# A streaming encoder step: gate operands one set ahead, sample rows in spent activations, native steps, third split buffers and a leaner scan

## The chip, the cores and the metric

The kernel is one program on one core of a Trainium2 chip. Its time is device microseconds of that core, from the launch to the end; a profiled execution also leaves a trace, whose span (first to last instruction) is a little shorter than the time. The engines are TensorE (PE; its weight loads are PEld), VectorE (DVE), ScalarE (ACT), GpSimd (POOL) and the queues that issue DMA (SP for plain loads and stores, POOL for gathers).

## What is computed

384 token rows (256 of a prompt, 128 of eight sample streams) of width 1024 go through two layers. Layer 0 mixes with a Mamba-2 scan in 8 groups of 4 heads, layer 1 with sliding-window attention; after each stands a PEER block, in which each token has 8 heads with 16 experts each out of 16384:

```
y = ssd_scan(xs, dt, A, B, C, state)                     # layer 0, per group
y = y + xs * d_skip                                      # one factor per head
y = rmsnorm(y * silu(z)) @ w_out
...
eid, gate = top16 of (q1 @ sub_k1 + q2 @ sub_k2)         # PEER, both layers
act = gelu(einsum('tkd,td->tk', u_tab[eid], x))
out = einsum('tk,tkd->td', gate * act, v_tab[eid])
```

## The kernel before

**Split products.** A float32 operand is cut in two fp32r parts: ScalarE casts raw to hi (L105), VectorE subtracts hi from raw into lo (L106). A product is three matmuls, hi x hi, hi x lo and lo x hi (`gemm_cols` L125, `gemm_rows` L134). raw has three buffers, hi and lo two each. A native product takes the float32 operands as they are; a native matmul is two instructions in the trace.

**The scan** (`mamba`, L209). For each of the 8 groups: four tiles of the input projection with their convolution (`conv_tile`), `decay`, `gate`, `tokens`; and, one group later, `states`, `outputs`, `turn` and `carry` of the group before. `outputs` adds the skip term xs * d_skip as a matmul with a diagonal tile dg (L483) into the same bank as the four head products (L487). `carry` adds each sample stream's new state: eight matmuls (L523) over 128 rows, each with a copy of B in which all but one stream's 16 rows are zero (`decay`, L453).

**The PEER block** (`peer`, L847) handles prompt tokens densely and sample tokens by gathers.
- 128 u steps (`u_step` L1130): step e2 loads 512 KB of the u table and writes gelu scores of 256 prompt tokens to G[e2 // 64][:, e2 % 64]. Steps in NATIVE (L47; only in the first 64) use raw and a float32 copy xf of the tokens. Beside the first 64 steps stands the routing (top 16 of the sub-key scores, on VectorE).
- Gates (`w_step` L1143): 32 sets for each half of G. A set builds one-hot operands ob, og and oa on VectorE and ScalarE, multiplies them (L1168) and scales G by the result (L1170). The sets of half 0 stand beside u steps 64 to 127, those of half 1 beside v steps 0 to 63.
- 128 v steps (`v_step` L1175): step e2 loads 512 KB of the v table, splits it and the scores (phi, plo), and adds 12 matmuls of 512 columns to four banks.
- Sample products (`u_item` L1104): for each of 128 columns of expert numbers a gather of 128 rows of u (512 KB) and a product with the sample rows xg on VectorE, at RATES (L54) per step in the three stretches of 64 steps.
- Quads (`v_quad` L1117): 32 quads of four gathered row sets of v; a quad is eight native matmuls on column tiles of 32 (L1126), one each 3.75 v steps from step 2 (QUADS). The gathered rows lie in seven buffers (gv, gath).
- At the end of the v steps h comes back from DRAM (L1265), for the residual sum.

What is written with `pin` keeps its order; the rest a scheduler puts in order per engine when the program is built. Each engine and each queue then runs its list in that order.

## Time and profile before

| | us |
|---|---|
| three runs | 2578.8, 2582.8, 2591.1 |
| median | 2582.8 |
| profiled execution, its own time | 2576.9 |
| its span | 2575.2 |
| TensorE busy | 2425.7 |
| VectorE busy | 1927.6 |
| ScalarE busy | 1313.5 |

The stages, in us from the span's start: scan and its output product to 401, queries of the first PEER block to 487, u steps to 715 and 927, v steps to 1175 and 1386, attention to 1561, and the second PEER block with queries to 1646, u steps to 1876 and 2087, v steps to 2343 and 2567. A stage is read by the busy time of its engines against its length: an engine whose busy time is the length sets it; where none is near, waits do.

### The profile page before, as it was taken

The numbers are of one execution on the slowest core, as the hardware profiler recorded it, in microseconds if no ns is written. First come the engines' busy times: TensorE is split into PE (matmuls) and PEld (weight loads), VectorE is DVE, ScalarE is ACT, GpSimd is POOL, SyncE is SP. The second block draws the span as 40 slices with busy tenths as digits, with TensorE's granted clock in tenths as the row PEclk, the third lists the DMA queues.
The fourth block names the chain that finished last, engine by engine and source line by source line (L and its number), as shares of the span: only waits on it lengthen the run. The fifth ranks groups of instructions, "written<-read, shape, count | busy, mean of one in ns | idle before, by whom it ended". The sixth has DMA issues, their size and how long they took to land. (4 is left out here: it accounts for less than half of the span.)

```text
span 2575.2 us, 45047 instructions
## 1 busy us (share of the span) xinstructions
PE 2425.7 (94%) x16816; PEld 2055.6 (80%) x16816; DVE 1927.6 (75%) x4206; ACT 1313.5 (51%) x2522; POOL 683.2 (27%) x749
## 2 busy tenths in 40 slices
PE   8999999999899999999998998999899999999998
PEld 7999988988789976666666878998789976667666
DVE  5877746989989988765455656989989988765445
ACT  5756524433456666554444544443456665554444
POOL 2222200033332244432331100033332244433331
PEclk9999999999999999999999989999999999999999
DMA  5545434478888899988886314478788898888886
GB/s 183 181 168 178 147 128 148 146 263 276 266 297 285 296 323 334 350 306 307 318 319 208 125 42 157 140 270 274 263 294 286 294 333 330 339 302 305 302 315 231
DMA packets 179117, 645.62 MB, mean 251 GB/s; under 512 B 24193, under 2 KB 26097, under 8 KB 176241
## 3 DMA queue, kind: packets, MB, share of 16 engines
q1 hardware_dynamic: 99632, 366.90, 40.6%
q0 software_dynamic: 79264, 275.84, 31.1%
q8 instruction: 132, 2.16, 0.3%
q14 instruction: 89, 0.72, 0.1%
HBM read 626.43 MB, written 18.06 MB: 250 GB/s over the span
## 5 line engine op out<-in xcount | busy, mean ns | idle before, releaser
L105 ACT CAST hi<-raw 128x1024 fp32r<-128x1024 f32 (+1 forms) x616 | 641.5, 1042 | 650.5 <-PE bank L131 425.7
L106 DVE TENSOR_TENSOR lo<-raw,hi 128x1024 fp32r<-128x1024 f32 (+1 forms) x616 | 750.0, 1218 | 234.3 <-ACT hi L105 233.2
L1072 POOL DMA_INDIRECT gath<-in_p_u,eidU x256 | 297.8, 1163 | 796.6 <-DVE gath L1109 424.0
L132 PE MATMUL bank<-xhi,lo 128*128 128x256 f32 (+1 forms) x1344 | 408.3, 304 | 12.6 <-DVE lo L106 12.5
L130 PE MATMUL bank<-xhi,hi 128*128 128x256 f32 (+1 forms) x1344 | 404.2, 301 | 4.2 <-ACT hi L105 4.2
L131 PE MATMUL bank<-xlo,hi 128*128 128x256 f32 (+1 forms) x1344 | 398.5, 297 | 0.0
L132 PE MATMUL bank<-qhi,lo 128*128 128x256 f32 (+1 forms) x1152 | 349.0, 305 | 29.7 <-DVE lo L106 29.5
L130 PE MATMUL bank<-qhi,hi 128*128 128x256 f32 (+1 forms) x1152 | 348.3, 303 | 19.6 <-ACT hi L105 12.0
L1109 DVE SCALAR_TENSOR_TENSOR gath<-gath,xg 128x1024 f32<-128x1024 f32 x256 | 311.8, 1218 | 50.2 <-DMA gath<-in_p_u,eidU 50.1
L131 PE MATMUL bank<-qlo,hi 128*128 128x256 f32 (+1 forms) x1152 | 344.3, 299 | 0.0
L143 PE MATMUL bank<-lo,phi 128*128 128x512 f32 x1024 | 331.6, 405 | 6.3 <-DVE lo L106 5.9
L143 PE MATMUL bank<-hi,plo 128*128 128x512 f32 x1024 | 322.7, 397 | 0.0
L143 PE MATMUL bank<-hi,phi 128*128 128x512 f32 x1024 | 291.6, 405 | 16.8 <-ACT hi L105 13.6
L105 ACT CAST phi<-G 128x256 fp32r<-128x256 f32 x256 | 103.4, 405 | 378.7 <-PE bank L143 264.9
L1072 POOL DMA_INDIRECT gv<-in_p_v,eidT x180 | 203.6, 1131 | 326.0 <-PE bank L1126 277.2
L132 PEld LDWEIGHTS bank<-xhi,lo 128*128 128x128 f32 x1344 | 255.4, 190 | 20.0 <-DVE lo L106 17.6
L143 PEld LDWEIGHTS bank<-hi,phi 128*128 128x128 f32 x1024 | 186.3, 189 | 96.4 <-ACT hi L105 41.0
L130 PEld LDWEIGHTS bank<-xhi,hi 128*128 128x128 f32 x1344 | 255.9, 190 | 8.8 <-ACT hi L105 5.2
L131 PEld LDWEIGHTS bank<-xlo,hi 128*128 128x128 f32 x1344 | 255.6, 190 | 0.3
L132 PEld LDWEIGHTS bank<-qhi,lo 128*128 128x128 f32 x1152 | 223.3, 195 | 36.5 <-DVE lo L106 36.2
L130 PEld LDWEIGHTS bank<-qhi,hi 128*128 128x128 f32 x1152 | 223.7, 194 | 23.5 <-ACT hi L105 15.1
L143 PEld LDWEIGHTS bank<-lo,phi 128*128 128x128 f32 x1024 | 187.2, 190 | 66.5 <-DVE lo L106 16.5
(343 smaller groups left out, 3889.1 us busy)
## 6 DMA issues: line engine op xcount, KB each, us to landing
raw<-in_u_t SPq DMA_DIRECT2D x256, 512.0 KB, 4.6
raw<-in_p_v SPq DMA_DIRECT2D x256, 512.0 KB, 5.5
raw<-in_w_in SPq DMA_DIRECT2D x32, 512.0 KB, 4.8
raw<-in_p_w_q SPq DMA_DIRECT2D x32, 512.0 KB, 5.5
s<-in_state_ssm SPq DMA_DIRECT2D x8, 1024.0 KB, 4.8
raw<-in_w_z SPq DMA_DIRECT2D x16, 512.0 KB, 3.8
out_sm_ssm<-s SPq DMA_DIRECT2D x8, 1024.0 KB, 4.2
raw<-in_w_out SPq DMA_DIRECT2D x16, 512.0 KB, 4.3
```

The lines of the kernel that those rows point to most:

```text
L105: act.copy(hi, raw)
L106: dve.tensor_tensor(lo, raw, hi32, op=OP.subtract)
L130: pe.matmul(ps, whi[:, s], xhi[:, k, c0:c1], start=(k == 0), stop=False)
L131: pe.matmul(ps, whi[:, s], xlo[:, k, c0:c1], start=False, stop=False)
L132: pe.matmul(ps, wlo[:, s], xhi[:, k, c0:c1], start=False, stop=(k == KD - 1))
L143: mm = pe.matmul(ps, x, w[:, hf * n:(hf + 1) * n], start=s_, stop=e_)
L1072: pool.indirect_dma_start(out=tile_, out_offset=None, in_=tab, in_offset=bass.IndirectOffsetOnAxis(ap=idx, axis=0))
L1109: pin(dve.scalar_tensor_tensor(tile_, tile_, 1.0, xg[g], op0=OP.mult, op1=OP.mult, accum_out=au[g][:, j:j + 1]))
```

## The change

- **Scan.** The skip term leaves TensorE: `tokens` writes xs * d_skip to y on VectorE, `outputs` adds the other terms to it, and dg is gone. `carry` takes B in two copies (streams of even and of odd number) and runs its eight matmuls on row tiles of 32 partitions, two streams each. `turn` and `carry` stand behind the x tiles, and some instructions are pinned.
- **u steps.** 18 native steps in place of 8 per layer (each third step from 3 to 54); a third hi and lo buffer up to step 55; the copies of the prompt's tokens spread over 8 steps. The rate of sample products is 0.75, 0.75 and 0.8 for 0.95, 0.8 and 0.8. The sample rows xg have one buffer: the second group's rows are loaded when the first group's 64 products are done.
- **Gates.** A set's operands are built one set ahead of its matmuls (`w_prepare`, `w_multiply`).
- **v steps.** 12 native steps (2, 7, ... 57), a third hi and lo buffer up to step 120, a third phi and plo. The gathered rows of v go to parts of G[0] that the v steps have used up, from step 18 on and up to 12 rows ahead. Quads stand at steps 24, 27, 30 and 33, and then two at a time each 6.45 steps. h is loaded by GpSimd's queue at step 121.

```
-TURN = 6
+TURN = 8
-NATIVE = range(4, 58, 7)
+NATIVE = range(3, 56, 3)
+NATIVE_V = range(2, 62, 5)
-RATES = (0.95, 0.8, 0.8)
-QUADS = (2, 3.75)
+W_FIRST = (0, 1)
+RATES = (0.75, 0.75, 0.8)
+QUADS = [24, 27, 30, 33] + [int(37 + 6.45 * (i // 2)) for i in range(28)]
...
+    more, turn_of = {}, {}
+    def ring(n, dt, tag, bufs):
+        if n == D and tag in more:
+            pl, extra = more[tag]
+            turn_of[tag] = (turn_of.get(tag, -1) + 1) % (bufs + extra)
+            if turn_of[tag] >= bufs:
+                return T(pl, [P, n], dt, tag=tag + "x", bufs=extra)
+        return T(stream, [P, n], dt, tag=tag, bufs=bufs)
     def load_raw(src, n=D):
-        raw = T(stream, [P, n], F32, tag="raw")
+        raw = ring(n, F32, "raw", 3)
...
-        hi = T(stream, [P, n], F32R, tag="hi", bufs=2)
-        lo = T(stream, [P, n], F32R, tag="lo", bufs=2)
+        hi = ring(n, F32R, "hi", 2)
+        lo = ring(n, F32R, "lo", 2)
...
-                        self.dg = T(two, [P, 2, P], F32, tag="dg", bufs=1)
-                        for j in range(2):
-                            pool.tensor_scalar(self.dg[:, j], ident, dsk[:, 2 * g + j:2 * g + j + 1], None, op0=OP.mult)
...
-                        self.Bt = Bt = T(two, [P, 2 + NSEQ, P], F32, tag="Bt", bufs=1)
+                        self.Bt = Bt = T(two, [P, 4, P], F32, tag="Bt", bufs=1)
                         act.copy(Bt[:, 0:2], pb[:, 0:2])
-                        for i in range(NSEQ):
-                            act.activation(Bt[:, 2 + i], pb[:, 2], AF.Copy, scale=seqm[:, i:i + 1])
+                        for w in range(2):
+                            act.activation(Bt[:, 2 + w], pb[:, 2], AF.Copy, scale=parm[:, w:w + 1])
...
+                            dve.tensor_tensor(heads(self.y[:, b]), heads(px),
+                                              dsk[:, self.hs].unsqueeze(2).to_broadcast([P, 4, 64]), op=OP.mult)
...
-                            for j in range(2):
-                                pe.matmul(o[:, j * P:(j + 1) * P], self.xs[:, j, b * P:(b + 1) * P], self.dg[:, j],
-                                          start=True, stop=False)
-                                for rr in (2 * j, 2 * j + 1):
-                                    cs = slice(64 * rr, 64 * rr + 64)
-                                    pe.matmul(o[:, cs], self.ab[:, rr, b], self.xdt[:, b, cs], start=False,
-                                              stop=(rr == 2 * j + 1))
+                            for rr in range(4):
+                                cs = slice(64 * rr, 64 * rr + 64)
+                                pe.matmul(o[:, cs], self.ab[:, rr, b], self.xdt[:, b, cs], start=True, stop=True)
...
-                        y12 = y[:, 1:].rearrange("p b (r d) -> p b r d", d=64)
-                        dve.tensor_tensor(y12, pO.rearrange("p b (r d) -> p b r d", d=64),
+                        y = self.y
+                        yo = T(two, [P, 2, 256], F32, tag="yo", bufs=1)
+                        dve.tensor_tensor(yo.rearrange("p b (r d) -> p b r d", d=64),
+                                          pO.rearrange("p b (r d) -> p b r d", d=64),
                                           etok[:, :, self.hs].unsqueeze(3).to_broadcast([P, 2, 4, 64]), op=OP.mult)
-                        dve.tensor_tensor(y[:, 0], self.zs[:, 0], pY[0], op=OP.mult)
+                        dve.tensor_tensor(y[:, 1:], y[:, 1:], yo, op=OP.add)
+                        dve.tensor_tensor(y[:, 0], y[:, 0], pY[0], op=OP.add)
                         dve.tensor_tensor(y[:, 1:], y[:, 1:], pY[1], op=OP.add)
-                        dve.tensor_tensor(y[:, 1:], y[:, 1:], self.zs[:, 1:], op=OP.mult)
+                        dve.tensor_tensor(y, y, self.zs, op=OP.mult)
...
-                        for i in range(NSEQ):
-                            pe.matmul(pss[i // 2][:, i % 2], self.Bt[:, 2 + i], self.xde[:, 2], start=True, stop=True)
+                        for w in range(2):
+                            for q in range(4):
+                                rows = slice(32 * q, 32 * q + 32)
+                                pin(pe.matmul(pss[q][:, w], self.Bt[rows, 2 + w], self.xde[rows, 2],
+                                              start=True, stop=True, tile_position=(32 * q, 0)))
...
-                    if g > 1:
-                        prev.turn()
                     G_.x_tile(0)
                     if g == 1:
                         prev.states()
                         prev.outputs()
+                    elif g:
                         prev.turn()
-                    if g:
                         prev.carry()
                     G_.x_tile(1)
+                    if g == 1:
+                        prev.turn()
+                        prev.carry()
...
-            xg = [T(x0ctx.__enter__(), [P, D], F32, tag="xg0"), T(one, [P, D], F32, tag="xg1")]
...
+            xg = {}
+            def load_group(g):
+                xg[g] = T(one, [P, D], F32, tag="xg", bufs=1)
                 rows = xrow[g]
                 pool.dma_start(xg[g], bass.AP(tensor=rows.tensor, offset=rows.offset, ap=[[0, GR], [D, TG], [1, D]]))
+            load_group(0)
...
-                    if done["u"] == P and n % 7 >= 4:
-                        tile_ = T(one, [P, D], F32, tag="gath", bufs=3)
-                    else:
-                        tile_ = T(pools["gv"], [P, D], F32, tag="gv", bufs=4)
+                    k = 4 * (n % (4 if n < 16 else 8 if n < 64 else 16))
+                    if k + 3 > e2 or holds.get(k, -1) >= 4 * done["v"]:
+                        return
+                    holds[k] = n
+                    done["f"] += 1
+                    tile_ = G[0][:, k:k + 4].rearrange("p e t -> p (e t)")
...
+                    if g + 1 < GR:
+                        load_group(g + 1)
...
+                ready.append((hf, t0, eg, oa))
+            def w_multiply():
+                hf, t0, eg, oa = ready.pop(0)
+                ps = bank([P, 8, HE])
+                for i in range(8):
+                    for j in range(2):
+                        pe.matmul(ps[:, i], oa[i // 4][:, i % 4], eg[:, i, j], start=(j == 0), stop=(j == 1))
...
+            def gates(hf, e2):
+                n = len(spread)
+                i = n - len(ready_for[hf])
+                if i < n and e2 >= W_FIRST[hf] + (i * 61) // n:
+                    ready_for[hf].pop(0)
+                    w_multiply()
+                    if i + 1 < n:
+                        w_prepare(hf, spread[i + 1])
+                    elif hf == 0:
+                        w_prepare(1, 0)
...
+                if e2 in NATIVE_V:
+                    raw = load_raw(vtab[e2])
+                    for b in range(2):
+                        for hf in range(2):
+                            pe.matmul(accs[b][hf], G[e2 // HE][:, e2 % HE, b * P:(b + 1) * P],
+                                      raw[:, hf * 512:hf * 512 + 512], start=False, stop=False)
+                    return
                 wt = load_split(vtab[e2])
-                phi = T(vpool, [P, NP], F32R, tag="phi", bufs=2)
-                plo = T(vpool, [P, NP], F32R, tag="plo", bufs=2)
+                phi = T(vpool, [P, NP], F32R, tag="phi", bufs=3)
+                plo = T(vpool, [P, NP], F32R, tag="plo", bufs=3)
...
-                while done["v"] < min(32, int((e2 - QUADS[0]) / QUADS[1] + 1)):
+                while done["v"] < 32 and QUADS[done["v"]] <= e2:
                     v_quad(done["v"])
                     done["v"] += 1
-                    ahead = 4 * done["v"] + (7 if done["u"] == P else 4)
-                    while done["f"] < min(ahead, P):
-                        fetch_v(done["f"])
-                        done["f"] += 1
+                if e2 >= 18:
+                    for _ in range(2):
+                        if done["f"] < 4 * done["v"] + 12:
+                            fetch_v(done["f"], e2)
...
+            lent = tc.tile_pool(name="pe0", bufs=1)
+            lpool = lent.__enter__()
+            more.update(hi=(lpool, 1), lo=(lpool, 1))
             for e2 in range(HE):
                 j = e2 - (HE - TURN)
                 if j == 0:
+                    more.clear()
+                    lent.__exit__(None, None, None)
...
-                if 0 <= j < 4:
-                    ks = slice(2 * j, 2 * j + 2)
-                    act.copy(xhi[:, ks], qhi[:, ks, :NP])
-                    act.copy(xlo[:, ks], qlo[:, ks, :NP])
                 u_step(e2)
+                if j >= 0:
+                    ks = slice(2 * (j // 2), 2 * (j // 2) + 2)
+                    x_, q_ = ((xhi, qhi), (xlo, qlo))[j % 2]
+                    pin(act.copy(x_[:, ks], q_[:, ks, :NP]))
...
+            w_prepare(0, 0)
...
-                if done["v"] == 32 and "gv" in pools:
-                    pools.pop("gv")
-                    gctx.__exit__(None, None, None)
+                if e2 == 2 * HE - 7:
+                    more.clear()
+                    lent.__exit__(None, None, None)
                     h = open_h()
-                    sync.dma_start(h, spill)
+                    pool.dma_start(h, spill)
```

Where the instructions stand now is shown at three places.

TensorE in the scan, `outputs` of one group before: dg is the skip term's diagonal, xdt and ab the head products, s the sample states, xhi and hi the next convolution.

```order
L483 MATMUL bank_1544<-dg_1125,xs_1233 128x128
L487 MATMUL bank_1544<-xdt_1466,ab_1121 128x64 x2
L483 MATMUL bank_1544<-dg_1125,xs_1233 128x128
L487 MATMUL bank_1544<-xdt_1466,ab_1121 128x64 x2
L490 MATMUL bank_1563<-st_1536,CT_1173 128x256
L494 MATMUL bank_1563<-s_193_1123,cm_54_246 32x256 x8
L130 MATMUL bank_1582<-xhi_100,hi_1585 128x384
```

And now, with the carry (L540) that follows two convolutions (48 matmuls, left out) later:

```order
L500 MATMUL bank_1517<-xdt_1439,ab_1108 128x64
L500 MATMUL bank_1518<-xdt_1439,ab_1108 128x64 x8
L502 MATMUL bank_1531<-st_1510,CT_1152 128x256
L506 MATMUL bank_1531<-s_194_1110,cm_55_247 32x256 x8
L144 MATMUL bank_1551<-xhi_100,hi_1554 128x384
...
L526 MATMUL bank_1650<-ident_69,y_1441 128x128 x3
L540 MATMUL bank_1657<-xde_1440,Bt_1342 128x256
L540 MATMUL bank_1658<-xde_1440,Bt_1342 128x256
L540 MATMUL bank_1659<-xde_1440,Bt_1342 128x256
L540 MATMUL bank_1660<-xde_1440,Bt_1342 128x256
L540 MATMUL bank_1657<-xde_1440,Bt_1342 128x256
```

The dg rows are gone, and the carry goes round four banks, one for each row tile, behind the transposes of y.

The queue of loads (SP) in the first u steps of the first PEER block before; in brackets the semaphores that a load waits for, the last one for the buffer (the engine that used it last).

```order
L114 DMA raw_5267<-in_u_t 128x1024 [waits DMAHW4_49,DVE_49]
L114 DMA raw_5299<-in_u_t 128x1024 [waits DMAHW3_49,PE_49]
L114 DMA raw_5331<-in_u_t 128x1024 [waits DMAHW5_49,DVE_49]
L114 DMA raw_5363<-in_u_t 128x1024 [waits DMAHW6_49,DVE_49]
L114 DMA raw_5401<-in_u_t 128x1024 [waits DMAHW7_49,DVE_49]
L114 DMA raw_5417<-in_u_t 128x1024 [waits DMAHW0_49,DVE_49]
```

And now:

```order
L128 DMA raw_5199<-in_u_t 128x1024 [waits DMAHW2_49,PE_49]
L128 DMA raw_5231<-in_u_t 128x1024 [waits DMAHW6_49,DVE_49]
L128 DMA raw_5243<-in_u_t 128x1024 [waits DMAHW7_49,DVE_49]
L128 DMA raw_5281<-in_u_t 128x1024 [waits DMAHW5_49,PE_49]
L128 DMA raw_5317<-in_u_t 128x1024 [waits DMAHW1_49,DVE_49]
L128 DMA raw_5347<-in_u_t 128x1024 [waits DMAHW2_49,DVE_49]
L128 DMA raw_5384<-in_u_t 128x1024 [waits DMAHW0_49,PE_49]
```

Each third load waits for TensorE in place of each seventh.

TensorE in the first half of the v steps, the first quad before: hi, lo, phi and plo are the v steps' operands, gv the gathered rows, cm the quad's factors, oa a gate set's weights.

```order
L143 MATMUL bank_10766<-hi_10889,phi_10893 128x512
L1126 MATMUL bank_10753<-gv_10761,cm_10869 32x512
L1126 MATMUL bank_10753<-gv_10759,cm_10869 32x512
L1126 MATMUL bank_10753<-gv_10757,cm_10869 32x512
L1126 MATMUL bank_10753<-gv_10755,cm_10869 32x512
L1126 MATMUL bank_10754<-gv_10761,cm_10869 32x512
...
L1168 LDWEIGHTS oa_10917
```

And the second quad now, with the gathered rows in G:

```order
L1153 MATMUL bank_10445<-G_620_3939,cm_11508 32x512
L157 MATMUL bank_10450<-hi_11522,phi_11526 128x512
L157 MATMUL bank_10451<-hi_11522,phi_11526 128x512
L1153 MATMUL bank_10445<-G_620_3939,cm_11508 32x512 x2
L157 MATMUL bank_10450<-lo_11523,phi_11526 128x512
...
L157 MATMUL bank_10453<-lo_11550,phi_11553 128x512
L1153 MATMUL bank_10445<-G_620_3939,cm_11508 32x512
L1153 MATMUL bank_10446<-G_620_3939,cm_11508 32x512 x4
L157 MATMUL bank_10452<-hi_11549,plo_11554 128x512
```

The quad stands in pieces of 1, 2 and 5 matmuls, with v matmuls between them; so do five of the first eight quads, and from the ninth on they stand whole, two at a time.

## Rows read from the trace of the kernel before

**Rows 1.** The page's busy times of each engine, their share of the span and the count of instructions.
```profile
PE 2425.7 (94%) x16816; PEld 2055.6 (80%) x16816; DVE 1927.6 (75%) x4206; ACT 1313.5 (51%) x2522; POOL 683.2 (27%) x749
```

**Rows 2.** Busy time of each engine by stage: the stretch, its length, then PE, PEld, DVE, ACT and POOL, each with its count of instructions, the granted clock as a share of full speed, the share of the DMA engines and their rate.
```profile
487.00:715.00 228.00, 207.12 (x1553) 198.78 (x1551) 203.09 (x649) 93.61 (x143) 67.86 (x50) 0.96 0.77 261
715.00:927.00 212.00, 204.57 (x2009) 199.39 (x2010) 197.82 (x303) 142.41 (x290) 56.09 (x55) 0.99 0.86 291
927.00:1175.00 248.00, 231.32 (x1505) 155.44 (x1506) 190.07 (x321) 141.24 (x278) 104.65 (x95) 0.99 0.91 333
1175.00:1386.00 211.00, 208.77 (x1010) 146.63 (x1009) 107.55 (x145) 92.50 (x130) 65.47 (x73) 1.00 0.85 304
1646.00:1876.00 230.00, 207.25 (x1563) 198.21 (x1561) 205.03 (x655) 95.22 (x146) 66.27 (x50) 0.97 0.75 258
1876.00:2087.00 211.00, 204.53 (x2008) 199.32 (x2008) 196.58 (x303) 141.12 (x287) 53.90 (x55) 0.99 0.87 292
2087.00:2343.00 256.00, 238.17 (x1527) 161.51 (x1528) 193.99 (x325) 144.00 (x283) 108.08 (x96) 0.98 0.89 328
2343.00:2567.00 224.00, 217.89 (x1039) 152.31 (x1037) 113.31 (x154) 95.67 (x136) 62.99 (x59) 0.99 0.83 291
```

**Rows 3.** A group of VectorE's instructions in the scan (count, busy us, mean ns, idle time before), and the busy times of 120 us of it (columns as in rows 2).
```profile
L463 DVE TENSOR_TENSOR xdt<-bank,dt 128x256 f32<-128x256 f32 x24 | 10.0, 419 | 14.6 <-PE bank L461 14.6
...
180.00:300.00 120.00, 120.00 (x844) 114.50 (x843) 93.99 (x156) 71.01 (x155) 32.52 (x64) 1.00 0.45 158
```

**Rows 4.** Timeline of TensorE in one group's `outputs`: start, time, line, operation, tiles, count of instructions.
```profile
179.50 0.44 PE L483 MATMUL bank<-dg,xs 128*128 128x128 f32 x2
179.78 0.56 PE L487 MATMUL bank<-xdt,ab 128*128 128x64 f32 x4
180.17 0.65 PE L490 MATMUL bank<-st,CT 128*128 128x256 f32 x2
180.75 1.07 PE L494 MATMUL bank<-s,cm 128*32 128x256 f32 x16
```

**Rows 5.** Timeline of TensorE: the carries of two groups in a row, the first with the row behind it, and in the attention the scores on tiles of 64 rows.
```profile
190.48 3.62 PE L523 MATMUL bank<-xde,Bt 128*128 128x256 f32 x16
193.93 0.60 PE L512 MATMUL bank<-ident,y 128*128 128x128 f32 x4
...
228.02 2.32 PE L523 MATMUL bank<-xde,Bt 128*128 128x256 f32 x10
...
1447.00 1.14 PE L727 MATMUL bank<-kT,qT 64*128 64x256 f32 x8
```

**Rows 6.** Timeline of TensorE in the u steps: the first and the last of 23 split matmuls in a row, a native step, and the split matmuls behind it.
```profile
489.95 0.28 PE L130 MATMUL bank<-qhi,hi 128*128 128x256 f32 x1
...
492.54 0.28 PE L131 MATMUL bank<-qlo,hi 128*128 128x256 f32 x1
492.65 3.62 PE L1135 MATMUL bank<-xf,raw 128*128 128x256 f32 x16
496.23 0.28 PE L130 MATMUL bank<-qhi,hi 128*128 128x256 f32 x1
```

**Rows 7.** VectorE's two largest groups of instructions from 487 to 715 us (count, busy us, mean ns, idle time before and what ended it).
```profile
L106 DVE TENSOR_TENSOR lo<-raw,hi 128x1024 fp32r<-128x1024 f32 x55 | 67.1, 1220 | 2.0 <-ACT hi L105 1.9
L1109 DVE SCALAR_TENSOR_TENSOR gath<-gath,xg 128x1024 f32<-128x1024 f32 x48 | 58.3, 1215 | 17.7 <-DMA gath<-in_p_u,eidU 17.7
```

**Rows 8.** The page's DMA issues: count, KB, median us from issue to landing.
```profile
raw<-in_u_t SPq DMA_DIRECT2D x256, 512.0 KB, 4.6
raw<-in_p_v SPq DMA_DIRECT2D x256, 512.0 KB, 5.5
```

**Rows 9.** Timeline of TensorE in the second half of the v steps: the first rows of two v steps in a row, and a quad's first row with that of the work behind it.
```profile
1201.48 1.09 PE L143 MATMUL bank<-hi,phi 128*128 128x512 f32 x4
...
1204.28 1.09 PE L143 MATMUL bank<-hi,phi 128*128 128x512 f32 x4
...
1207.17 0.62 PE L1126 MATMUL bank<-gath,cm 128*32 128x512 f32 x2
...
1209.03 1.21 PE L143 MATMUL bank<-hi,phi 128*128 128x512 f32 x4
```

**Rows 10.** Groups of instructions from 927 to 1175 us, the first half of the v steps: the gathers by table and buffer, and the subtractions on VectorE of the scores' split.
```profile
L1072 POOL DMA_INDIRECT gv<-in_p_v,eidT x56 | 63.5, 1134 | 87.4 <-PE bank L1126 74.6 <-issue 10.1 <-PE bank L143 1.5
L106 DVE TENSOR_TENSOR plo<-G,phi 128x256 fp32r<-128x256 f32 x62 | 26.2, 422 | 24.6 <-PE bank L143 18.0 <-PE bank L1168 3.7 <-ACT phi L105 2.5
L1072 POOL DMA_INDIRECT gath<-in_p_u,eidU x25 | 26.9, 1075 | 24.6 <-DVE gath L1109 14.5 <-DMA gv<-in_p_v,eidT 5.9 <-issue 4.0
L1072 POOL DMA_INDIRECT gath<-in_p_v,eidT x14 | 14.2, 1017 | 23.6 <-PE bank L1126 19.5 <-issue 2.7 <-DVE gath L1109 1.0
```

**Rows 11.** Waits from 487 to 715 us: who waited for whom, us in total, times, longest (of ScalarE, TensorE and the queue of loads).
```profile
ACT hi L105 <- DMA raw<-in_u_t: 15.5, 8, 3.9
PE bank L130 <- ACT hi L105: 6.2, 8, 1.5
SPq L114 <- PE bank L1135: 11.6, 6, 3.0
```

**Rows 12.** Busy times and transfer rates in stretches of the first half of the v steps (columns as in rows 2).
```profile
936.00:1079.00 143.00, 128.30 (x821) 85.57 (x819) 115.12 (x196) 78.05 (x154) 69.21 (x62) 0.98 0.95 353
1040.00:1053.00 13.00, 12.57 (x62) 8.61 (x60) 9.00 (x15) 5.15 (x8) 7.74 (x7) 1.00 1.02 398
```

54 lines of the change are left out of this document (25 added, 29 removed).

## The prediction

> **What bounds the kernel now.** I read the busy times first [rows 1]: TensorE is busy for 94% of the span, VectorE for 75%. So a gain has to come out of TensorE's own work, or out of the 150 us in which it stands still. The table by stage [rows 2] says where that is, with a granted clock of 0.96 or more in each (1 is 2.4 GHz). The first half of the u steps (487 to 715, and 1646 to 1876 in the second layer) has it at 207 of 228 and 230, with VectorE at 203 and 205: VectorE is the bound there, and TensorE waits. The second half of u has TensorE at 204.5 of 212 and 211. The first half of the v steps has 231 of 248 and 238 of 256, at 333 and 328 GB/s, the highest rates of the table; the second half of v is TensorE alone (209 of 211). In the scan TensorE is busy for 120 of 120 us [rows 3].
>
> The profiled execution took 2576.9 us, 2 us below the lowest of the three runs (median 2582.8). The sum is made against 2576.9 and read as a time of the same kind.
>
> **The scan.** Per group, six dg matmuls go from TensorE, and the eight carry matmuls become row tiles of 32 partitions. In the timeline [rows 4] a dg matmul (two instructions) and four xdt instructions take 0.67 us (179.50 to 180.17), the four alone 0.39, so a dg costs 0.28: 48 x 0.28 = 13.4 us. The carry holds TensorE for 3.45 us (190.48 to 193.93) with 16 instructions, and comes again 37.5 us later, the length of a group [rows 5]. No row shows 32-row tiles. The nearest are eight instructions on 64-row tiles in two positions, 1.14 us at 1447.00, where the carry's pitch of 0.216 would give 1.7; and the 16 on 32-column tiles, 1.07 us at 180.75. The xdt instructions, each with 128 columns of weights of its own, show 0.10 us for one, and the carry keeps 128 columns of weights, so I take 16 x 0.10 = 1.6 us (bounds 1.0 and 3.45, no tile beside another): 8 x 1.85 = 14.8 us. The TensorE page of the Trainium skill (TensorE: Matmul & The Clock Gate, "Measured speedup vs the span model") gives 3.07 times for four row tiles; by that the carry would be 1.1 us, and the sum 4 us lower. No run here shows it yet.
>
> Against these 28.2 us stands VectorE. A group gets three more products over 256 columns (0.42 each [rows 3]), one more sum over 512 and a last product over 768 in place of 512 (estimates of 0.69 and +0.35 from the 0.42): 2.3 us. It is busy 94 of 120 us now, 29.4 in a group of 37.5 us; then 31.7 in some 34, 93%. The second half of u has VectorE at 93% and TensorE at 96.5% [rows 2], so I give back 3.5% of 8 x 34 us: 9.5. Scan: **-19 us** (bounds -33 and -4). The six fewer copies on ScalarE (59% busy in this stretch) and the dg products on GpSimd lie beside this and count nothing. The carry and transposes stand together in the new order, with operands that are a whole convolution old; the pins cost nothing there.
>
> **First half of u.** 10 more native steps per layer (18 for 8). A split step issues a matmul every 0.118 us, 24 are 2.83; a native one takes 492.65 to 496.23 less one split matmul, 3.46 [rows 6]. That is 0.63 more on TensorE. On VectorE each saves a subtraction of 1.22 us, 12.2 us, and the lower rate (0.75 for 0.95 over some 53 steps) moves 10 sample products of 1.22 to the v steps: 203 becomes 179. With its 17.7 us of waits for gathers [rows 7] it needs at most 197. TensorE: 0.96 x 207.1 = 198.8 us of full clock, of which 56 x 2.83 + 8 x 3.46 = 186.2 are steps and 12.6 the routing. After: 46 x 2.83 + 18 x 3.46 + 12.6 = 205.1. TensorE becomes the bound, and without idle time that is 23 and 25 us less: **-48 us**.
>
> **Second half of u.** TensorE's work stays; it idles 7 us per layer. Operands one set ahead and three fewer products take some of that. The single xg buffer adds a load behind product 63: VectorE has seven other instructions (some 5 us) in the new order before product 64, and a load of that size lands in 4.6 to 5.5 us [rows 8], so it costs about nothing; if the load lands late, VectorE's splits stand behind it, some us once a layer. **-6 us** for both layers (bounds -14 and +6).
>
> **The v steps.** Twelve native steps: four matmuls of two instructions of 0.43 us (twice the 0.216 for 256 columns), 3.43, for 2.80 split [rows 9], an estimate of +0.63 each, 7.6 us. Two quads of 1.86 us move from the first half to the second. Five quads now stand in pieces of 1, 2 and 5 among the v matmuls; a whole one runs four tiles at a time in four turns of 0.43, the pieces in 2 + 2 + 4 turns, so 5 x 1.7 = 8.5 us. First half: 231.3 + 7.6 - 3.7 + 8.5 = 243.7; second: 208.8 + 3.7 = 212.5; together 456.2 for 459. In the second layer 238.2 and 217.9 give 250.6 + 221.6 = 472.2 for 480. If no idle time is left (VectorE's 190 us there change by +14 x 1.22 for products and -12 x 1.64 for splits [rows 7, 10], to 187): **-11 us**. The reload of h moves from the load queue behind the gathers; it is needed at the same place as before, and I count nothing.
>
> Sum so far: 19 + 48 + 6 + 11 = 84 us, 2493.
>
> **What this leaves out: a raw buffer held by TensorE.** A split step gives its raw buffer back when VectorE has read it; a native one when TensorE has done the step. The queue of loads is in order: the load that waits for TensorE holds those behind it. The trace shows it at work: that queue waits six times for the native matmuls, 11.6 us, and ScalarE eight times for a raw load, 15.5 us, in a stage with eight native steps [rows 11]. TensorE itself waits eight times for hi, 6.2 us. So a native step costs between 0 and 15.5 / 8 = 1.94 us of idle TensorE, 0.78 by its own waits. In u each third step is native now and its buffer is always the same one: 5.7 us from the end of one native step to the next one's start, for a load of 4.6. In v, two steps of 243.7 / 64 give 7.6 us for a load of 5.5 and a cast [rows 8]. Third hi and lo buffers lengthen the lead. I take 0.6. Of these steps there are (18 + 12) x 2 = 60, and the sum above counts none of their waits: **+36 us**. 2493 + 36 = **2529**.
>
> **The rivals.**
> *The buffers hide it all.* The native price is near 0 and TensorE runs without gaps: 2493, and to 2480 with the carry at its lower bound and the rest of the scan's loss gone. For: the third buffers, and rows in the second half of u that keep TensorE at 96%. Against: the order of loads, whose bursts of three after a native step share the engines with gathers.
> *Transfers bind the first half of v.* It moves 64 raw loads and 95 gathers now [rows 10]; then 64, 39 for u and 68 for v (12 rows ahead of the 14 quads): 171 x 0.524 = 89.7 MB. My 243.7 + 12 x 0.6 = 251 us needs 357 GB/s. The busiest stretch had 353 over 143 us, with a piece of 398 [rows 12]; at the 333 of today's half it would take 269: +37 us over both layers, 2566. The gathers have 12 rows of lead that can slip. The Trainium skill (DMA: Bandwidth & Descriptors, "Where 436 GB/s comes from") names about 358 GB/s from HBM for one core. By that this half would take 250 us; the piece of 398 goes beyond it for 13 us, the mean of the stretch doesn't.
> *The held buffer at its full price (slower).* At 1.94 us for each of 60 native steps, 116 us stand against 84: 2609. It decides from 84 / 60 = 1.4 us per step on. For: that each native step in the trace already makes ScalarE wait. Against: TensorE's own waits are 40% of ScalarE's, and the third sets exist.
> *Row tiles that don't run together.* The change would then not do what it says: the carry stays at 3.45, +15, 2544. This lies in my range.
>
> **How the numbers follow.** My forecast, 2505 to 2555 with the last rival in it: 0.53. No hold: 0.20. Transfers: 0.17, the time between 2555 and 2585. The held buffer at over 1.4: 0.10. The range 2485 to 2582 leaves out about a tenth at the top and some hundredths below. A measurement of this kernel tells about 0.5% from no change, 12.9 us here, so faster is below 2570: 0.53 + 0.20 + 0.07 = 0.80. Same, up to 2596: the rest of the transfers and some of the held buffer, 0.12. Slower: 0.08.
>
> **What would show it.** Scan: a group near 34 us in place of 37.5, the 16 carry instructions in 1.0 to 2.1 us, VectorE at 90% or more. First half of u: 210 to 218 us, VectorE below 185 busy; ScalarE's waits for raw loads per native step, near 0.6 us of them on TensorE. First half of v: near 250 us and 355 GB/s, quads in pieces at 0.86 us. It is wrong if the stages with native steps don't shorten, if the load queue waits for TensorE more than 1.4 us per native step, or if the scan's VectorE holds TensorE up by more than 1.2 us in a group.

## The result, and the profile after

| | before | changed |
|---|---|---|
| runs, us | 2578.8, 2581.2, 2582.8, 2591.1 | 2609.6, 2616.7, 2618.4, 2626.3 |
| median, us | 2582.0 | 2617.6 |
| profiled execution, its own time, us | 2576.9 | 2626.3 |

The ratio is 1.0147, with a 95% interval of 1.0116 to 1.0178: the changed kernel is slower by 1.5%, where the forecast had it 1.9% faster (2529 for the profiled 2576.9). Between chips the time of the kernel before moves by half a per cent (medians of 2569.6 to 2582.0 us here), so experiments are compared by their ratio to it on their own chip.

The busy times by stage of the changed kernel (columns as in [rows 2]; the scan, the four halves of u and v of the first layer, then those of the second):

```profile
0.00:403.00 403.00, 365.36 (x2360) 330.93 (x2361) 286.39 (x500) 202.41 (x404) 68.66 (x165) 0.97 0.45 157
497.00:719.00 222.00, 207.72 (x1457) 197.15 (x1456) 188.19 (x636) 81.32 (x135) 49.18 (x41) 0.97 0.73 245
719.00:939.00 220.00, 205.20 (x2033) 201.53 (x2031) 192.22 (x293) 143.61 (x292) 49.28 (x50) 0.98 0.82 274
939.00:1203.00 264.00, 246.56 (x1406) 153.49 (x1407) 185.50 (x320) 123.16 (x255) 116.62 (x102) 0.97 0.88 323
1203.00:1425.00 222.00, 216.99 (x1079) 151.64 (x1079) 108.68 (x151) 89.33 (x131) 70.47 (x82) 0.99 0.84 314
1691.00:1905.00 214.00, 200.28 (x1427) 190.78 (x1426) 185.08 (x617) 81.00 (x134) 52.31 (x41) 0.98 0.73 250
1905.00:2127.00 222.00, 206.03 (x2034) 202.09 (x2033) 192.55 (x295) 143.97 (x294) 49.96 (x50) 0.97 0.82 271
2127.00:2385.00 258.00, 242.72 (x1403) 151.06 (x1404) 185.11 (x319) 121.39 (x251) 117.52 (x102) 0.99 0.91 333
2385.00:2606.00 221.00, 216.15 (x1077) 149.91 (x1076) 109.31 (x149) 89.33 (x130) 67.05 (x66) 1.00 0.85 316
```

A better table for the cause splits each stage in three: time without any TensorE instruction (idle), half of TensorE's busy time at the lower clock level, 1.2 GHz (lost), and the rest (work at 2.4 GHz). It is worked out from TensorE's instructions and the stretches of granted clock; a stage ends here with the last lo product of the scan's output, with a ScalarE activation of a u step, or with a cast of v's scores, so its ends differ by some us from those of [rows 2]. Where two lengths stand, they are those of the two layers, and the other columns are sums over both.

| us | length before | changed | idle before | changed | lost before | changed |
|---|---|---|---|---|---|---|
| scan and its output product | 398.9 | 403.0 | 14.4 | 37.6 | 3.4 | 9.3 |
| queries | 89.0 | 94.1 | 5.5 | 9.2 | 2.4 | 4.3 |
| u, first halves | 222.8 + 222.3 | 221.7 + 213.8 | 41.8 | 28.0 | 14.6 | 10.3 |
| u, second halves | 215.6 + 216.1 | 220.1 + 221.5 | 14.9 | 30.2 | 3.4 | 3.8 |
| v, first halves | 253.9 + 256.0 | 263.7 + 258.5 | 34.9 | 33.2 | 8.5 | 10.0 |
| v, second halves | 212.1 + 216.6 | 221.2 + 221.1 | 7.3 | 9.9 | 1.7 | 1.7 |
| attention, second queries | 256.4 | 267.5 | 21.4 | 22.5 | 11.6 | 17.7 |
| sum | 2559.7 | 2606.1 | 140.2 | 170.7 | 45.7 | 57.1 |

TensorE's work rose by 4.5 us (2373.8 to 2378.3): 25 less in the scan (381 to 356), 23 more in the v steps, 9 more in the first halves of u, and the rest in small amounts. The kernel is slower above all because TensorE stands still for 30 us more, and at the lower clock loses 11 more; the scan and the second halves of u have most of it. (This profile is the slowest of the four runs; that of the last experiment, a run of the same kernel with a span of 2600.5 us, has 153.7 idle, 49.3 lost, 2379.2 work.)

Where TensorE stands still, from the timeline of the changed kernel (start, time, engine, line; in brackets the idle time before it and what ended it):

```profile
73.17 0.34 DVE L451 SCALAR_TENSOR_TENSOR ab<-ab,acum,msk 128x128 f32<-128x128 f32 x1
...
76.72 1.75 DVE L459 TENSOR_TENSOR ab<-ab,bank 128x1536 f32<-128x1536 f32 x1 [1.92 <-ACT ab L454]
...
78.62 5.36 PE L500 MATMUL bank<-xdt,ab 128*128 128x64 f32 x24 [10.19 <-DVE ab L459]
...
163.67 1.15 PE L540 MATMUL bank<-xde,Bt 32*128 32x256 f32 x16
164.75 0.44 PE L144 MATMUL bank<-xhi,hi 128*128 128x384 f32 x1
...
172.77 2.47 DVE L543 TENSOR_TENSOR s<-s,bank 128x512 f32<-128x512 f32 x4
...
173.50 0.39 PE L438 MATMUL bank<-hi,xhi 128*128 128x256 f32 x1 [1.73 <-DVE s L543]
...
364.67 0.70 PE L540 MATMUL bank<-xde,Bt 32*128 32x256 f32 x4
...
403.58 0.69 PE L540 MATMUL bank<-xde,Bt 32*128 32x256 f32 x2
...
404.63 1.13 PE L540 MATMUL bank<-xde,Bt 32*128 32x256 f32 x10
...
412.90 1.51 PE L904 MATMUL bank<-ident,qTp 128*128 128x128 f32 x6 [6.71 <-DVE qTp L895]
...
827.12 0.86 POOL L917 DMA_DIRECT2D xg<-xrow  x1 [5.54 <-DVE gath L1134]
...
844.04 1.23 DVE L1134 SCALAR_TENSOR_TENSOR gath<-gath,xg 128x1024 f32<-128x1024 f32 x1 [11.66 <-DMA xg<-xrow]
...
847.94 0.58 PE L146 MATMUL bank<-xhi,lo 128*128 128x256 f32 x1 [9.27 <-DVE lo L109]
```

Read it from the bottom. The load of the second group's sample rows is issued at 827.12 and lets VectorE's product 64 start at 844.04, 16.9 us later; VectorE runs in order, so the subtractions behind that product are late, and TensorE stands for 9.27 us (10.34 in the second layer). At 403.58 and 404.63 stand twelve of the sixteen instructions of the last group's carry, 39 us behind the first four (364.67) and among the last products of the output; the queries then start after a gap of 6.7 us, where the kernel before has gaps of 0.17 to 0.33 us (below). At 173.50 the gate waits for a bank that the carry holds until VectorE has added it. At 78.62 TensorE has waited 10.19 us for group 0's decay: of its twelve instructions L451, eleven ran from 57.72 on and the first one, which is pinned, at 73.17.

The same place in the kernel before, the last product of the scan's output and the first transposes of the queries:

```profile
399.40 0.63 PE L143 MATMUL bank<-hi,ylo 128*128 128x512 f32 x2
399.86 0.60 PE L887 MATMUL bank<-ident,qTp 128*128 128x128 f32 x4
400.64 0.33 PE L887 MATMUL bank<-ident,qTp 128*128 128x128 f32 x1 [0.17 <-DVE h L600]
401.29 0.49 PE L887 MATMUL bank<-ident,qTp 128*128 128x128 f32 x2 [0.33 <-DVE h L600]
```

### The profile page after: what moved, and what is told of

The parts are those of the page before. It is cut to its first block, busy times and chain, and to the rows that moved or that the text cites. A ratio compares the mean times of both kernels' runs of the same rounds, so it can differ in the third digit from the quotient of the medians.

```text
span 2624.6 us, 43859 instructions
## 1 busy us (share of the span) xinstructions
PE 2444.5 (93%) x16462; PEld 2031.6 (77%) x16464; DVE 1883.9 (72%) x4171; ACT 1236.9 (47%) x2410; POOL 661.7 (25%) x735
## 4 chain that ended last, share of the span: by engine, by line
PE 57%; DVE 17%; DMA 12%; issue 9%; ACT 3%; POOL 2%; another core or an unknown queue 0%; SPq 0%; POOLq 0%; DVEq 0%; ACTq 0%
PE bank L157 24%; PE bank L146 6%; PE bank L144 6%; PE bank L145 6%; PE bank L1153 5%; DVE lo L109 4%; DMA raw<-in_u_t 4%; PE bank L1234 2%; DVE gath L1134 2%; DMA ab<-acum_rows 2%; PE bank L1204 2%; ACT hi L108 2%; DMA gath<-in_p_u,eidU 2%; DMA raw<-in_p_v 1%; POOL gath L1093 1%
## 5 line engine op out<-in xcount | busy, mean ns | idle before, releaser
L108 ACT CAST hi<-raw 128x1024 fp32r<-128x1024 f32 (+1 forms) x474 | 492.3, 1040 | 662.6 <-PE bank L145 304.3
L109 DVE TENSOR_TENSOR lo<-raw,hi 128x1024 fp32r<-128x1024 f32 (+1 forms) x474 | 573.4, 1212 | 229.1 <-ACT hi L108 213.8
L1093 POOL DMA_INDIRECT G<-in_p_v,eidT x256 | 276.9, 1081 | 357.2 <-PE bank L1153 228.8
L144 PE MATMUL bank<-qhi,hi 128*128 128x256 f32 (+1 forms) x792 | 247.3, 313 | 12.0 <-ACT xf L906 6.4
L146 PE MATMUL bank<-qhi,lo 128*128 128x256 f32 (+1 forms) x792 | 242.2, 307 | 12.6 <-DVE lo L109 12.4
L109 DVE TENSOR_TENSOR plo<-G,phi 128x256 fp32r<-128x256 f32 x232 | 97.5, 422 | 210.2 <-PE bank L157 162.6
L145 PE MATMUL bank<-qlo,hi 128*128 128x256 f32 (+1 forms) x792 | 241.4, 305 | 0.0
L157 PE MATMUL bank<-lo,phi 128*128 128x512 f32 x636 | 205.4, 404 | 11.5 <-DVE lo L109 8.4
L157 PE MATMUL bank<-hi,plo 128*128 128x512 f32 x636 | 201.5, 398 | 0.0
L1190 ACT ACTIVATE oa<-ioh,e2T 128x128 f16<-128x128 f16 x512 | 162.7, 390 | 45.2 <-PE bank L1204 39.6
```

The source lines that it names most:

```text
L108: act.copy(hi, raw)
L109: dve.tensor_tensor(lo, raw, hi32, op=OP.subtract)
L144: pe.matmul(ps, whi[:, s], xhi[:, k, c0:c1], start=(k == 0), stop=False)
L145: pe.matmul(ps, whi[:, s], xlo[:, k, c0:c1], start=False, stop=False)
L146: pe.matmul(ps, wlo[:, s], xhi[:, k, c0:c1], start=False, stop=(k == KD - 1))
L157: mm = pe.matmul(ps, x, w[:, hf * n:(hf + 1) * n], start=s_, stop=e_)
```

## The experiments

Theory A: the time is lost at a few long waits that the change made. Theory B: native steps cost it, by the raw buffer that they hold. Theory C came with the fifth run. [changed] stands for the changed kernel, whose ratio is 1.0147 (1.0135 when it was run again at the end); a gain in us is worked out from the ratios to these two.

**Sample rows ready early.** The rows lie in columns of G[1] that are not yet in use, and a ScalarE copy brings them to xg.
```
+load_rows(1, G[1][:, HE - 4:])            # at u step 64, GpSimd's queue
-pool.dma_start(xg[1], ...)                # behind product 63
+act.copy(xg[1], G[1][:, HE - 4:])
```


> The second group's sample rows are loaded into unused columns of G[1] at u step 64, and one ScalarE copy brings them to xg when product 63 is done, so that no product waits for a transfer. Theory A (the changed kernel loses its time at a few long waits, each followed by a stretch at half the clock): the two TensorE gaps of 9.3 and 10.3 us in the second half of u go, and most of the 10.2 and 13.7 us at half clock behind them; 19 to 31 us less than the changed kernel's 2617.6, 2587 to 2599 us. Theory B (native steps that hold their raw buffer cost the time): TensorE waits elsewhere for the same loads, 2610 to 2618 us.


1.0084 (1.0063 to 1.0106), 2596.7 us. That lies inside A's range of times, but the kernel before is 9 us faster on this chip too; by the ratios the gain is 13 to 16 us, short of A's 19. And its profile has the second halves of u at 218.6 and 219.4 us, hardly shorter: the gaps at product 64 are gone, and new ones of 5.2 and 8.0 us stand behind step 64, where the load now holds up the gathers.

**First decay free.**
```
-(pin if rr + b == 0 else lambda i_: i_)(dve.scalar_tensor_tensor(ab...
+(pin if rr + b == 0 and g else lambda i_: i_)(dve.scalar_tensor_tensor(ab...
```


> The pin on the first decay instruction of group 0 is taken away, all other pins stay; VectorE then has all twelve in a row, and the product with the exponent ahead of the next convolution. Theory A: the gap of 10.2 us before the first head products goes, with the 20 us at half clock around it; 10 to 20 us less, 2598 to 2608 us. Theory B: 2614 to 2620 us. In the profile the scan and its output product take 386 to 396 us in place of 405.7.


1.0073 (1.0045 to 1.0102), 2595.2 us: by the ratios 16 to 19 us less, inside A's 10 to 20. The scan takes 392.3 us in place of 403.0. The 10 us gap is gone; one of 7.1 us is left in front of group 0's transposes (TensorE's timeline of this run):
```profile
75.00 0.34 PE L146 MATMUL bank<-xhi,lo 128*128 128x384 f32 x1
82.48 1.51 PE L526 MATMUL bank<-ident,y 128*128 128x128 f32 x6 [7.14 <-DVE y L517]
```

**Eight native u steps.** `NATIVE = range(4, 58, 7)`.


> Eight native u steps per layer as before in place of 18; all else as in the changed kernel. Theory B: each of 20 native steps fewer gives back 0.63 us of TensorE and 0.6 to 1.9 us of idle time, 25 to 50 us less, 2568 to 2593 us. Theory A with VectorE as the bound of the first half of u: 20 subtractions of 1.2 us more on VectorE against 12.6 us less on TensorE, between 2612 and 2640 us.


1.0099 (1.0074 to 1.0124), 2599.9 us, between the theories. The first halves of u take 206.3 and 204.7 us for 221.7 and 213.8: 24.5 us for 20 steps, 1.2 each, of which the trace puts 0.5 to work and 0.7 to idle time and the lower clock. The second halves take 7 us more each; why was not looked into.

**No native v steps.** `NATIVE_V = ()`.


> No native v steps; all else as in the changed kernel. Theory B: 24 native steps fewer give back 0.63 us of TensorE and 0.6 to 1.9 us of idle time each, 30 to 60 us less, 2558 to 2588 us. Theory A: TensorE's 15 us come back in part, against 24 more splits of 1.6 us on VectorE; 2600 to 2620 us.


1.0108 (1.0087 to 1.013), 2602.1 us: 0.3 to 0.4 us for a step, less than B and inside A's range.

**Both waits gone**, the sample rows by the queue of plain loads.


> Both long waits are taken out of the changed kernel: the first decay of group 0 is free of its pin, and the second group's sample rows come by the queue of plain loads into unused columns of G[1], with one ScalarE copy to xg when product 63 is done (by the gathers' queue, as in the run before, the load held up the gathers behind it by 5 and 8 us). Theory A: both effects add, 0.74% for the first and 0.63% to 1.0% for the second; a ratio to the kernel before of 0.997 to 1.002. Theory B: 1.004 or more.


1.012 (1.010 to 1.0139): A's range (up to 1.002) is missed, and B's (1.004 or more) holds, but not for B's reason. The scan has its 10 us (393.0), the second halves of u have nothing (220.4 and 221.2): wherever this load stands, what is queued behind it waits, now the u table, with gaps of 10.1 and 11.3 us. That leads to theory C: the transfer itself is slow. TensorE's timeline of this run, behind the load at u step 64:
```profile
731.96 0.58 PE L144 MATMUL bank<-xhi,hi 128*128 128x256 f32 x1 [10.10 <-ACT hi L108]
```

**Both waits gone, 8 native u steps and none in v** (the first), **18 and none** (the second).


> As the run with both waits gone, and with 8 native u steps per layer as before and none in v. Theory B on top of A (a native step costs about 0.5 us net in u and 0.9 in v, as the stages of two runs show): 20 x 0.5 + 24 x 0.9 = 32 us less than with the waits gone, a ratio of 0.985 to 0.992. If VectorE is the bound once the waits are gone, its 44 more splits take that back: 0.997 to 1.005.

> As the run with both waits gone, with 18 native u steps and none in v. It splits the difference between the two runs before: by the stages of the earlier runs v's share is 22 of 32 us, a ratio 0.8% below the run with the waits gone; if VectorE binds the v steps once the products of the first half of u lie there, no gain.


1.0047 (1.003 to 1.0064) and 1.0107 (1.0078 to 1.0136): the first lies in its second branch (0.997 to 1.005), the second shows no clear gain over the 1.012 of the run before. By the ratios the ten more native u steps of each layer cost 0.6%, those in v 0.1%, too little to tell.

**Fourth raw buffer.**
```
-more.update(hi=(lpool, 1), lo=(lpool, 1))
+more.update(raw=(lpool, 1), hi=(lpool, 1))      # u and v
```


> The changed kernel with a fourth raw buffer in place of the third lo buffer, in the u steps up to 55 and the v steps up to 120. Theory B (native steps hold their raw buffer, and the queue of loads stands behind it): ScalarE's waits for raw loads in the first half of u (82 us) fall by half, and the kernel gains 10 to 25 us, a ratio of 1.005 to 1.011. If the held buffer isn't what native steps cost: 1.012 to 1.018.


1.0179 (1.0162 to 1.0196): the second branch as a whole, but the two stages part. The first halves of u fall to 209.3 and 209.7 us, and the v steps grow by 19 us over both layers. That is not idle time (36 us for 43): the matmuls of the quads, which stand in more pieces there, are busy for 22 us more over both layers. These are the quads' busy times in the v steps of the first layer (the stretch, its length, PE, PEld, clock, DMA share and rate), in the changed kernel and in this run:
```profile
939.00:1425.00 486.00, 71.46 (x512) 16.24 (x512) 0.98 0.86 319
927.00:1416.00 489.00, 84.41 (x512) 17.24 (x512) 0.99 0.86 316
```

**The load of xg in two.**
```
-pool.dma_start(xg[g], bass.AP(..., ap=[[0, GR], [D, TG], [1, D]]))
+for q in range(GR):
+    pool.dma_start(xg[g][q * TG:(q + 1) * TG], bass.AP(..., ap=[[D, TG], [1, D]]))
```


> The changed kernel, but the load of xg is written as two transfers of 64 rows each in place of one with an outer dimension of 2. Theory C (the transfer itself is what costs: written with two entries outermost it ends at 49 to 57 GB/s with a tenth of the DMA engines at work, and holds up whatever queue it stands in): it lands in 5 to 8 us in place of 17, VectorE waits for it under 3 us, the TensorE gaps of 9.3 and 10.3 us go, and the second halves of u take 206 to 213 us in place of 220 and 221.5; a ratio of 1.005 to 1.010. If 512 KB by this queue take their time however they are written: the gaps stay and the ratio is 1.012 to 1.017.


1.0078 (1.0051 to 1.0104), as C said. The page's DMA issues of the kernel before (count, KB, median us from issue to landing):
```profile
xg<-xrow POOLq DMA_DIRECT2D x4, 512.0 KB, 20.7
```
and of this one, with its second halves of u (columns as in [rows 2]):
```profile
xg<-xrow POOLq DMA_DIRECT2D x8, 256.0 KB, 4.2
```
```profile
719.00:927.00 208.00, 203.31 (x2033) 199.77 (x2031) 191.85 (x293) 143.49 (x292) 49.19 (x51) 1.00 0.87 291
1874.00:2083.00 209.00, 204.02 (x2037) 200.40 (x2034) 193.33 (x297) 143.76 (x293) 51.98 (x51) 1.00 0.87 288
```
The same bytes, now as two loads, land in 4.2 us each, TensorE idles 5 us in each of these halves, and they are 7 us shorter than before the change.

**Scan order**, with the load in two and the first decay free: carry ahead of turn, group 0's turn behind the gate.


> The load of xg in two transfers, the first decay of group 0 free of its pin, and in the scan the carry ahead of the transposes of y (turn), for group 0 with the transposes behind the gate. Theory A: the 7 us gap ahead of group 0's transposes, which was left when the pin was gone, goes too; the scan takes 380 to 387 us in place of 392 to 393, and the ratio is 0.996 to 1.002. If the wait only moves to the gate's banks: 390 or more, 1.000 to 1.006.


1.0024 (1.0002 to 1.0045), and the scan at 392.3 us as without the new order: the second branch. The gap of 7 us is gone, and 1.5 to 2.9 us per group stand before the transposes of B, which wait for VectorE's part of turn.

**The same with a fourth raw buffer in u only**, and **without native v steps.**


> As the run before, with a fourth raw buffer in place of the third lo buffer in the u steps up to 55 only. Theory B for u: the first halves of u, 222 and 214 us in the changed kernel, take 208 to 211, as in the run with the fourth raw buffer in both; 0.5% to 0.7% below the run before, a ratio of 0.990 to 0.996. If that run's short halves were chance: no difference.

> As the run before, without native v steps. If these cost 0.4 to 0.9 us each, 10 to 22 us less, a ratio 0.4% to 0.8% below the run before; if VectorE's 24 more splits bind the first half of v, no gain.


0.9953 (0.9928 to 0.9978) and 0.9958 (0.9926 to 0.9991): the first as expected, with first halves of u of 208.4 us in both layers; in the second no gain, so native v steps cost nothing that shows here. ScalarE's waits for raw loads in the first half of u, of the changed kernel:
```profile
ACT hi L108 <- DMA raw<-in_u_t: 58.3, 14, 7.9
ACT hix L108 <- DMA raw<-in_u_t: 23.8, 8, 8.0
```
and with four raw buffers there (rawx is the fourth):
```profile
ACT hi L108 <- DMA raw<-in_u_t: 37.0, 10, 8.0
ACT hi L108 <- DMA rawx<-in_u_t: 20.6, 4, 6.8
ACT hix L108 <- DMA raw<-in_u_t: 8.0, 4, 3.9
ACT hix L108 <- DMA rawx<-in_u_t: 2.5, 2, 1.4
```
82.1 us became 68.1: they fell by a sixth, not by half as theory B had it, and yet the halves of u are 18 us shorter over both layers (434.9 to 416.8).

From here on each run changes one thing in the version of 0.9953. **Quads later** (8 and 24 in the halves of v), **the scaling of the states on GpSimd**, **8 native u steps.**


> The version with two-part xg load, free first decay, carry ahead of the transposes and fourth raw buffer in u (0.9953 of the kernel before), with 8 quads in the first half of v and 24 in the second, in place of 14 and 18. The work of TensorE is the same. If transfers hold TensorE in the first half (24 row sets of v fewer are gathered there, 12.6 MB of 85), its idle time falls from 14 to 20 us to under 10 and the sum of both halves by 8 to 10 us per layer: a ratio of 0.987 to 0.992. If gates and native steps hold it, both halves together stay, 0.994 to 0.997.

> The same version with the product of the sample states by their decay (2.28 us of VectorE per group) on GpSimd. If VectorE's load is what keeps the scan at 37 us per group, it falls by 1 to 2 us per group: the scan takes 378 to 386 us in place of 392, a ratio of 0.989 to 0.993. If it is the order in which VectorE comes to the adds that free the carry's banks, or GpSimd is later than VectorE: 390 to 400 us, 0.995 or more.

> The same version with 8 native u steps per layer in place of 18. If native steps relieve VectorE as the forecast had it, the first halves of u grow from 208 to 212 to 220 us, a ratio of 0.998 to 1.003. If TensorE is the bound there with either, they shrink by up to 6 us each, 0.990 to 0.994; if both effects cancel, 0.994 to 0.997.


0.9995 (0.9969 to 1.0021): the halves of v in the first layer go from 254.5 and 216.8 us to 236.6 and 239.2, their sum doesn't fall, and the first half still idles 10.7 us at a lower rate of transfers (in the version without the later quads it idles 9 us in this layer and 15 in the second, not the 14 to 20 of the expectation). Transfers are not what holds it. Its two halves of v, columns as in [rows 2]:
```profile
910.00:1146.00 236.00, 225.30 (x1338) 146.76 (x1339) 185.10 (x314) 121.87 (x252) 98.68 (x86) 1.00 0.88 318
1146.00:1386.00 240.00, 234.28 (x1149) 153.12 (x1148) 109.81 (x153) 89.14 (x132) 90.81 (x96) 1.00 0.88 332
```
The scaling on GpSimd: 1.0018 (0.9998 to 1.0038), the second branch; GpSimd takes 3.62 us where VectorE takes 2.28, and the scan grows to 409 us, beyond both. Eight native u steps: 0.995 (0.9932 to 0.9968), no difference to 18. The first halves of u are a little shorter (206 and 203 us for 208), the second ones longer (212 for 210 and 209).

The first halves of u of four runs make a square, in us over both layers (what else differs between these runs lies outside this stage, but for the third lo buffer, whose place the fourth raw buffer takes):

| | three raw buffers | four |
|---|---|---|
| 18 native steps | 435 ([changed]) | 417 |
| 8 native steps | 411 | 408 |

A fourth raw buffer gives 18 us with 18 native steps and 3 with 8. So it is the native steps that need it, which is what theory B says, for u alone.

**The last carry bank by bank**, and **[changed] again** on that chip.
```
-for w in range(2): for q in range(4): ...                  # four banks in turn
+for q in range(4): for w in range(2): ...                  # last group only
```


> The version with two-part xg load, free first decay, carry ahead of the transposes and fourth raw buffer in u, with the eight carry matmuls of the last group held bank by bank (both streams of a bank, then the next) in place of four banks in turn. Six banks hold the output product there. If the held order over four banks is what lets twelve of its sixteen instructions run only behind the output product, the gap of 6.7 us ahead of the queries' transposes falls to under 2 us, the stage from 97.5 to 89 to 93 us, and the ratio is 0.991 to 0.995. If the queries wait for something else: the gap stays, 0.994 to 0.997.

> The changed kernel as it is, on the same chip as the run before: a ratio of 1.011 to 1.018 to the kernel before, as measured first. Below 1.010, the single effects named so far are too large.


0.9915 (0.989 to 0.9941), 2547.1 us for 2571.7: the queries take 88 us for 97.5, and their transposes start without the gap:
```profile
395.16 0.60 PE L905 MATMUL bank<-ident,qTp 128*128 128x128 f32 x4
395.93 0.33 PE L905 MATMUL bank<-ident,qTp 128*128 128x128 f32 x1 [0.18 <-DVE h L620]
396.59 0.48 PE L905 MATMUL bank<-ident,qTp 128*128 128x128 f32 x2 [0.33 <-DVE h L620]
```
[changed]: 1.0135 (1.0105 to 1.0165). Its two first halves of v, columns as in [rows 2]:
```profile
935.00:1187.00 252.00, 241.51 (x1405) 151.23 (x1406) 186.40 (x320) 123.23 (x255) 116.27 (x102) 0.99 0.91 336
2110.00:2360.00 250.00, 239.91 (x1403) 149.52 (x1404) 185.49 (x319) 122.20 (x254) 120.66 (x102) 1.00 0.92 344
```

## Why the prediction was wrong, by its own steps

By its own terms the forecast adds 17 us to TensorE's work (28 less in the scan, 13 more in u, 32 more in v) and still shortens the kernel by 48, so it takes 65 us out of TensorE's idle time and time at the lower clock; in the trace these grew by 42. The terms of work came out near or on the safe side: 25 less in the scan, 9 more in the first halves of u, 23 more in v.

- **Second half of u: the step that failed most clearly.** The forecast has "a load of that size lands in 4.6 to 5.5 us [rows 8], so it costs about nothing". The rows were those of another transfer of the same size; the page of the kernel before has a row for the very load, 20.7 us, which nothing there waited for. Term -6, measured +10; the load in two gives 0.6 to 0.7% of the kernel (1.0147 or 1.0135 to 1.0078), and then the halves are 7 us shorter each than before the change.
- **Scan: "the pins cost nothing there", and 9.5 us given back.** The work came out nearly as computed: 25 us less for 28. The sixteen carry instructions take 1.08 us (163.67 to 164.75) for 3.45, 3.2 times faster, so row tiles do run together. By the 3.07 times of the Trainium skill (TensorE: Matmul & The Clock Gate, "Measured speedup vs the span model") they would take an estimated 1.1 us, nearer than my 1.6. But 29 us of idle and lost time came against the 28, not 9.5: a pin on one instruction 14 us, by its gap of 10 and half of the 8 us at 1.2 GHz behind it (7 to 11 us of the scan come back without it: 399.4 and 403.0 to 392.3), then 1 to 2 us in each group at banks that wait for VectorE's adds. VectorE's busy time per group came out as computed (31.4 us from 127 to 312 us, for 31.7), but in groups of 37.0 us, not 34, so it is busy for 85% of them, not 93%. What is late is then single instructions in its order and not its load; this is read from the waits, each of which ends with one VectorE instruction, and the run with the scaling on GpSimd can't decide it, since GpSimd takes longer. Term -19, measured +4; in the best version -5.
- **Queries: not in the sum.** The held order over four banks met a place where six banks are taken. The stage is 5 us longer in the changed kernel; with the other waits gone the repair gives 0.38%.
- **First half of u: the hold was sized about rightly, the gain that it was set against was too large.** 0.6 us of idle time per native step was taken; eight in place of 18 steps show 0.7 of idle and lost time, beside 0.5 of work. (The queue of loads names TensorE for 7.1 us of its waits in the first of these halves, 0.4 for a native step; the hold is read not from that row but from the square of runs above.) But the -48 counts on "without idle time", which takes away all of the 56 us of idle and lost time that these halves had; with the fourth raw buffer 21 of them are left, and the halves are 28 us shorter than before the change. VectorE's busy time fell to 188 and 185 us and not to 179, but its relief adds nothing to the gain: with four raw buffers 8 and 18 native steps idle for 18 and 19 us and give the same time (0.9950, 0.9953). With the eight native steps of before the rest of the change gives 34 us (445 to 411); how much of it is the lower rate of products was not tried alone. Term -48 and +22 of the 36, measured -10.
- **v steps.** Their work grew by 23 us, less than the 32 of the terms (native steps and quads in pieces). But their idle time was written off (the prediction has "If no idle time is left") and stayed: 42 us before and 43 in this profile, most of it in the first halves, and 31 in that of the last experiment. Native steps are not its cause in the repaired version, transfers neither. What it is stays open. Term -11 and +14, measured +26 in this profile and +8 in that of the last experiment.

Of the rivals, the held buffer came nearest in time (2609) and not in its mechanism: 1.94 us per step was never seen. That it came near is luck. The transfers' rival had the first half of v at 269 us for 333 GB/s, and this profile's 264 and 258 us at 323 and 333 GB/s look like it. But the same kernel takes 252 and 250 us at 336 and 344 GB/s in the last experiment, so 333 is no bound, and with the later quads idle time doesn't follow the bytes. The halves of v shown here move 314 to 344 GB/s. None reaches the about 358 GB/s that the Trainium skill (DMA: Bandwidth & Descriptors, "Where 436 GB/s comes from") names for one core.

The repairs add up: 0.6 to 0.7% for the load (to 1.0078), 0.5% for the free first decay with the new scan order (to 1.0024), 0.7% for the fourth raw buffer in u (to 0.9953) and 0.4% for the last carry (to 0.9915). So the changed kernel holds a faster one than the kernel before, by 0.9% (0.6 to 1.1), behind four waits. That the forecast's 2529 (0.981) isn't reached is above all the scan's 14 us. The attention, which the change leaves alone, is 11 us longer in the changed kernel: 1 idle, 6 at the lower clock and 4 of work; that wasn't pursued.

## What to carry to other kernels

A buffer that is taken away turns a transfer that nothing waited for into one on the path: look up that transfer's own row, not one of the same size. An order held by hand has to be followed to where it meets scarce buffers or late operands, the first and the last round of a loop above all. Idle time that a change doesn't remove by name should stay in the sum.

## What the hardware showed that was not expected

A load of 512 KB whose pattern has two entries outermost landed in 20.7 us in the median of the kernel before and in 16.9 in the changed one, there in its last 6 us (838 to 844) at 49 to 53 GB/s with 12 to 13% of the DMA engines busy. By an estimate, two engines busy out of the sixteen would be 12.5%; the trace doesn't tell which engines worked. Written as two loads of 256 KB with 64 entries outermost the same bytes landed in 4.2. It isn't the size of a load alone, since plain loads of 512 KB land in 4.6 [rows 8]. Moved to another queue, the slow form held that queue up, with gaps of 10 and 11 us on TensorE. Why the form matters was not tried further.
